# Weight splits for attention during the projections, and context attention's first products ahead of x's Fourier input

## The chip, the cores and the metric

The kernel runs on one core of one Trainium2 chip. The metric is the device time of one execution in microseconds (us), the median of several. The engines are TensorE (PE, matmuls), VectorE (DVE), ScalarE (ACT), GpSimd (POOL) and SyncE (SP), which in this kernel issues all transfers through one queue, in order.

## The reference

Two layers of a hybrid block work on 512 tokens x and 256 context tokens ctx, model width 1024. In each layer a modulated input goes through one projection of 1440 columns, and the columns go to four groups: latent attention (MLA), spatial gating, multi-scale pooling and Fourier mixing. The results are joined and go through an output projection, a residual layer norm and a SwiGLU network. Context tokens use the same weights but see only themselves; in the second layer they supply only keys and values. Cut to what matters here:

```python
cq = rms_norm(proj[..., OFF_Q:OFF_KV], q_norm)
ckv = rms_norm(proj[..., OFF_KV:OFF_KR], kv_norm)
q = (cq @ w_uq).reshape(B, L, N_HEADS, QK_NOPE + QK_ROPE)      # 8 heads, 64 + 32
k_nope = (ckv @ w_uk).reshape(B, L, N_HEADS, QK_NOPE)
v = (ckv @ w_uv).reshape(B, L, N_HEADS, V_DIM)
...
attn = blocked_attend(q, concat([k_c, k]), concat([v_c, v]))
mix = concat([attn, spatial_gating(...), multiscale_pool(...), fourier_mix(...)])
if not last:
    attn_c = attend(q_c, k_c, v_c)
    mix_c = concat([attn_c, ...])
```

Everything is float32 and the order of the groups within a layer is free, as long as what they read is there.

## The kernel before

A product in float32 accuracy is made of three matmuls in a rounded format (`mm3`, L172 to L174). For that every operand is split into a high and a low part: ACT casts the value (L168), and DVE, for some tiles POOL, subtracts that from the value (L169). A weight tile comes into a staging tile `s` (pool `sp`, four buffers), usually 512 KB, and is split into a tile `w` (pool `wp`, five buffers). A staging buffer is free when the subtraction has read it; a `w` buffer when the last matmul has read it.

The program is written as a sequence of stages, and a planner orders the instructions of each engine; every engine then works strictly in that order. In the first layer `inproj` makes the first products (its last columns are the queries' and keys' latents, `at`). `chunk_b` projects the two halves of spatial gating: accumulators `pd` and `ps`, then a layer norm on DVE of the second half (L374 and L376 statistics, L530 and L533 scaling, L169 the split of the result) with small steps on POOL between. `chunk_d` projects the pooling group with the weight halves D0 and D4 (named by the first k tile of each), `chunk_c` the Fourier group with C0 and C4, context tokens first, then x. Then come `pool_sums` on DVE and POOL, `spatial` (transposes L819, products, and L814, which multiplies the gate), `pool_proj`, and attention.

Beside this runs the computation of the next modulation (`mods`): 512 KB tiles of `w_mod` are loaded into the same four staging buffers (L260) and multiplied, unsplit, with the condition vectors (L274, four matmuls of each 128 rows of `w_mod`), then follow a sum with the bias (L280), transposes (L293) and copies into `modT` (L298, L300). Its instructions are put among the other matmuls by `fill`. A tile of `w_mod` keeps its staging buffer until its L274 matmuls are done.

`qkv_weights` (L605 to L624) loads `w_uk` and `w_uv` into one staging tile and the two halves of `w_uq` into two more, scales them by the norm's gains (L607, L617), splits them and copies parts of the query weights on POOL (L624). The three `w` tiles stay in use until attention ends. `make_ckv` and `make_cq` transpose and split the latents, `make_k` and `make_q` make keys of a head pair and the query of a head, `values` the values. `attention` is a generator that yields after each step of one head: `scores`, the keys of the next pair, the query of the next head, the transposes of an earlier step (`turn`) and the weighted sum of one still earlier (`weigh`). In layer 0 attention of the context runs interleaved with the generator `fourier`. `chunk_c` was called as a function, and `fill(99)` runs out what is left of `mods`.

## Time and profile before

| | us |
|---|---|
| median of three runs | 1672.93 (1671.89 to 1675.65) |
| the profiled execution | 1668.66 |
| its span | 1666.9 |
| PE busy | 1572.3 (94%) |
| DVE busy | 1045.8 (63%) |
| ACT busy | 769.3 (46%) |
| POOL busy | 260.6 (16%) |
| mean granted clock | 0.984 |

PE is busy in nearly all of the span, but busy time of pipelined matmuls overlaps, so what counts in a stretch is where PE stands and what it then waits for. The timeline shows it: an instruction's row ends with the idle time ahead of it and its releaser. The stretch of layer 0 that matters here lies from 100 to 245 us, that of layer 1 from 1056 to 1110 us. Times of starts are counted from the span's start.

### The profile page before, as it was taken

What the parts mean: (1) busy time and instruction counts of PE and PEld (TensorE: products, weight loads), DVE (VectorE), ACT (ScalarE), POOL (GpSimd) and SP (SyncE); (2) the same over time, 40 slices, a digit from 0 to 9 for tenths busy, and PEclk for the clock granted to TensorE, in tenths of its full rate; (3) what the DMA queues carried; (4) which work ended last, traced back from release to release, by engine and by line L of the source; (5) the groups of instructions that cost most, each with busy time, mean ns of one, the idle gap of its engine ahead of it and who ended that gap; (6) DMA issues with size and microseconds to landing.
All of it is one profiled execution on the core that took longest, in us unless ns stands there. A gap on an engine that the chain in (4) does not pass through costs nothing.

```text
span 1666.9 us, 23834 instructions
## 1 busy us (share of the span) xinstructions
PE 1572.3 (94%) x9129; PEld 1358.9 (82%) x9129; DVE 1045.8 (63%) x1591; ACT 769.3 (46%) x1371; POOL 260.6 (16%) x322
## 2 busy tenths in 40 slices
PE   6999889999999999999999798989999899998997
PEld 3856778888899999997766487879988899997786
DVE  1443676876766666664544437677857778886835
ACT  2521675884633434344232516368845445554220
POOL 0213011330000000000305005433311000001402
PEclk9999999999999999999999799999999999999999
DMA  9566114128322333449876726411156244457321
GB/s 327 178 218 202 39 39 140 46 81 279 110 82 93 94 95 101 130 133 338 315 257 226 222 67 200 145 33 39 39 176 197 76 127 127 127 177 266 119 82 58
DMA packets 180502, 241.80 MB, mean 145 GB/s; under 512 B 10874, under 2 KB 127468, under 8 KB 180388
## 3 DMA queue, kind: packets, MB, share of 16 engines
q1 hardware_dynamic: 180388, 240.28, 44.8%
q8 instruction: 72, 1.18, 0.3%
q14 instruction: 42, 0.34, 0.1%
HBM read 215.30 MB, written 24.94 MB: 144 GB/s over the span
## 4 chain that ended last, share of the span: by engine, by line
PE 81%; DVE 8%; DMA 4%; ACT 4%; issue 2%; SPq 0%; POOL 0%; POOLq 0%; DVEq 0%; ACTq 0%
PE pd L1187 21%; PE pd L172 10%; PE pd L173 10%; PE pd L174 10%; PE ps L172 5%; PE ps L173 5%; PE ps L174 5%; PE ps L1187 4%; PE ps L274 3%; PE ps L731 3%; PE ps L715 2%; DVE w L169 2%; DVE u L169 2%; DMA u<-in_w_mod_dram 1%; DMA s<-in_w_ffn_dram 1%
## 5 line engine op out<-in xcount | busy, mean ns | idle before, releaser
L168 ACT CAST w<-s 128x1024 fp32r<-128x1024 f32 (+3 forms) x285 | 292.7, 1031 | 473.0 <-PE pd L1187 141.2
L169 DVE TENSOR_TENSOR w<-s,w 128x1024 fp32r<-128x1024 f32 (+3 forms) x285 | 352.5, 1244 | 195.8 <-ACT w L168 195.7
L1187 PE MATMUL pd<-u,w 128*128 128x256 f32 (+1 forms) x1938 | 295.4, 308 | 19.0 <-DVE w L169 14.3
L1187 PEld LDWEIGHTS pd<-u,w 128*128 128x128 f32 x1938 | 282.7, 191 | 25.2 <-DVE w L169 15.8
L172 PE MATMUL pd<-w,u 128*128 128x512 f32 (+5 forms) x728 | 277.9, 383 | 8.3 <-DVE u L169 3.6
L173 PE MATMUL pd<-w,u 128*128 128x512 f32 (+5 forms) x728 | 274.3, 377 | 1.7 <-DVE w L169 1.7
L174 PE MATMUL pd<-w,u 128*128 128x512 f32 (+5 forms) x728 | 272.9, 376 | 0.0
L172 PEld LDWEIGHTS pd<-w,u 128*128 128x128 f32 x728 | 140.3, 193 | 54.6 <-issue 16.3
L173 PEld LDWEIGHTS pd<-w,u 128*128 128x128 f32 x728 | 140.3, 193 | 29.3 <-issue 5.9
L174 PEld LDWEIGHTS pd<-w,u 128*128 128x128 f32 x728 | 140.2, 193 | 27.2 <-issue 4.2
L168 ACT CAST u<-y 128x512 fp32r<-128x512 f32 (+2 forms) x178 | 94.2, 546 | 61.5 <-DMA y<-yd 28.4
L169 DVE TENSOR_TENSOR u<-y,u 128x512 fp32r<-128x512 f32 (+2 forms) x118 | 77.7, 679 | 63.0 <-ACT u L168 61.8
L169 POOL TENSOR_TENSOR u<-y,u 128x512 fp32r<-128x512 f32 (+1 forms) x60 | 78.9, 1323 | 225.5 <-ACT u L168 203.2
L172 PE MATMUL ps<-u,w 128*128 128x256 f32 (+2 forms) x288 | 92.1, 328 | 1.8 <-DVE modT L300 1.1
L174 PE MATMUL ps<-u,w 128*128 128x256 f32 (+2 forms) x288 | 93.5, 327 | 0.0
L173 PE MATMUL ps<-u,w 128*128 128x256 f32 (+2 forms) x288 | 93.3, 326 | 0.1
L172 PE MATMUL ps<-w,u 128*128 128x512 f32 (+1 forms) x208 | 81.2, 398 | 5.6 <-DVE u L169 4.7
L169 DVE TENSOR_TENSOR u<-ps,u 128x512 fp32r<-128x512 f32 (+2 forms) x106 | 66.7, 654 | 28.8 <-ACT u L168 27.8
L173 PE MATMUL ps<-w,u 128*128 128x512 f32 (+1 forms) x208 | 82.0, 395 | 1.4 <-DVE w L169 1.4
L174 PE MATMUL ps<-w,u 128*128 128x512 f32 (+1 forms) x208 | 81.4, 393 | 0.0
L1304 POOL TENSOR_TENSOR f<-f,f 128x1024 f32<-128x1024 f32 x10 | 25.8, 2598 | 333.5 <-DMA f<-rd 254.4
L1187 PE MATMUL ps<-u,w 128*128 128x384 f32 (+1 forms) x456 | 75.3, 313 | 0.0
(250 smaller groups left out, 2579.5 us busy)
## 6 DMA issues: line engine op xcount, KB each, us to landing
s<-in_w_ffn_dram SPq DMA_DIRECT2D x154, 512.0 KB
s<-in_w_out_dram SPq DMA_DIRECT2D x50, 512.0 KB
u<-in_w_mod_dram SPq DMA_DIRECT2D x48, 512.0 KB
s<-in_w_mod_dram SPq DMA_DIRECT2D x48, 512.0 KB
s<-in_w_in_dram SPq DMA_DIRECT2D x16, 512.0 KB
yd<-f SPq DMA_DIRECT2D x19, 384.0 KB
y<-yd SPq DMA_DIRECT2D x88, 64.0 KB
y<-yd SPq DMA_DIRECT2D x22, 256.0 KB
```

Source lines behind the costliest of these rows:

```text
L168: A_.copy(out=hi, in_=src)
L169: (eng or V_).tensor_tensor(out=lo, in0=src, in1=f(hi), op=ALU.subtract)
L172: T_.matmul(ps, lhsT=ll, rhs=rh, start=start, stop=False)
L173: T_.matmul(ps, lhsT=lh, rhs=rl, start=False, stop=False)
L174: T_.matmul(ps, lhsT=lh, rhs=rh, start=False, stop=stop)
L274: T_.matmul(ps[32 * j:32 * j + 32, :n], lhsT=sst[:, k, :], rhs=ws[j // 2][:, (j % 2) * n:(j % 2 + 1) * n], start=(k == 0), stop=(k == KD - ...
L715: T_.transpose(pt[:, o:o + P], es[t2][:, k * P:(k + 1) * P], ident)
L731: T_.matmul(av[:, 0:256], lhsT=vt[k][:, h, :], rhs=pts[k // 2][:, a, (k % 2) * 256:(k % 2 + 1) * 256], start=(k == 0 and a == 1), stop=(k ...
L1187: T_.matmul(ps, lhsT=A[u][:, k], rhs=B[k][:, v], start=first and k == 0 and i == 0, stop=last and k == 3 and i == 2, skip_group_check=True)
L1304: G_.tensor_tensor(out=y, in0=y, in1=bc[0], op=ALU.mult)
```

## The change

Three edits. First, `wkv, wq = qkv_weights(l)` is called straight behind `chunk_b`, ahead of `chunk_d`, in both layers; before, it came behind `make_ckv`. Second, `chunk_c` becomes a generator that yields after each stream. In layer 0, when the context's part is done, `make_cq(C)` is called, context attention is created and its first part runs: the keys of the first pair and the first two queries. Only then follows x's part of `chunk_c`, and then `fill(99)`. Third, the generator of context attention makes its queries two heads ahead, and yields once more, behind these first products. Lines behind the edits have moved down (L607 is L608, L617 is L618, L814 is L820, L866 is L872).

```diff
@@ chunk_c
             v = lambda ap: ap.rearrange("p n c -> p (n c)")
             split(v(st.f[0]), v(st.f[1]), pd[:, :n])
+            yield
@@ attention
         make_k(0, wkv, st)
         q[0] = make_q(st, 0, wq)
+        qa = 1
+        if st.s:
+            q[1] = make_q(st, 1, wq)
+            qa = 2
+            yield
         for i, (h, qp) in enumerate(steps):
...
-            if qp == 0 and h < NH - 1:
-                q[h + 1] = make_q(st, h + 1, wq)
+            if qp == 0 and h < NH - qa:
+                q[h + qa] = make_q(st, h + qa, wq)
@@ hybrid_kernel, the loop over layers
         chunk_b(l, act)
+        wkv, wq = qkv_weights(l)
         pts = chunk_d(l, act)
...
         make_ckv(C, at)
         if l == 1:
             make_ckv(X, at)
-        wkv, wq = qkv_weights(l)
+        vt = []
         if l == 1:
             make_cq(X, at)
-        chunk_c(l, act)
+        cc = chunk_c(l, act)
+        if l == 0:
+            next(cc)
+            make_cq(C, at)
+            ac = attention(C, vt, wkv, wq)
+            next(ac)
+        run(cc)
         fill(99)
-        if l == 0:
-            make_cq(C, at)
-        vt = []
         fo = fourier(l, act)
         if l == 0:
             values(wkv, vt, range(NTC))
-            ac = attention(C, vt, wkv, wq)
```

Where the instructions went, by the order that the planner gives each engine. SP in layer 0, the transfers at the end of `chunk_b`, before (`s` is a staging buffer with its tile's number, `in_w_in` the input projection's weights: D4, C0 and C4):

```order
L260 DMA s_138_940<-in_w_mod_dram 128x1024
L186 DMA s_159_1040<-in_w_in_dram 128x4x256
L186 DMA s_161_1045<-in_w_in_dram 128x4x256
L186 DMA s_163_1050<-in_w_in_dram 128x4x256
L260 DMA s_169_1074<-in_w_mod_dram 128x1024
L286 DMA gd<-y_1057 2x512 x2
```

and now:

```order
L606 DMA s_159_1040<-in_w_uk_dram 128x512
L607 DMA s_159_1040<-in_w_uv_dram 128x512
L615 DMA s_161_1047<-in_w_uq_dram 128x768
L615 DMA s_164_1063<-in_w_uq_dram 128x768
L186 DMA s_167_1079<-in_w_in_dram 128x4x256
L186 DMA s_169_1084<-in_w_in_dram 128x4x256
L243 DMA y_1107<-in_b_mod_dram 2x512
L286 DMA gd<-y_1096 2x512 x2
L243 DMA y_1107<-in_b_mod_dram 2x512 x3
L872 DMA y_1406<-in_w_pool_dram 64x64 x4
L186 DMA s_171_1089<-in_w_in_dram 128x4x256
L260 DMA s_177_1113<-in_w_mod_dram 128x1024
```

Three transfers of attention weights stand ahead of D4, and the next `w_mod` tile stands behind C4 instead of behind three transfers. DVE at the same place, from the last statistics of `chunk_b` on (`i` and `pd`, `ps` are its tiles and accumulators), before:

```order
L376 BN_AGGR st_1031<-bn_1029 128x2
L530 SCALAR_TENSOR_TENSOR i_968<-pd_731,st_1006,y_964 128x256
L530 SCALAR_TENSOR_TENSOR i_1016<-ps_732,st_1020,y_964 128x256
L530 SCALAR_TENSOR_TENSOR i_1016<-ps_733,st_1031,y_964 128x256
L533 SCALAR_TENSOR_TENSOR i_968<-i_968,st_1006,y_964 128x256
L533 SCALAR_TENSOR_TENSOR i_1016<-i_1016,st_1020,y_964 128x256
L533 SCALAR_TENSOR_TENSOR i_1016<-i_1016,st_1031,y_964 128x256
```

and now, with the scalings (L618) and subtractions (L169 from `s_161` and `s_164`) of the query weights, and D4's from `s_167`:

```order
L618 TENSOR_SCALAR s_161_1047<-s_161_1047,st_1049 128x768
L530 SCALAR_TENSOR_TENSOR i_968<-pd_731,st_1006,y_964 128x256
L618 TENSOR_SCALAR s_164_1063<-s_164_1063,st_1065 128x768
L530 SCALAR_TENSOR_TENSOR i_1016<-ps_732,st_1020,y_964 128x256
L530 SCALAR_TENSOR_TENSOR i_1016<-ps_733,st_1031,y_964 128x256
L169 TENSOR_TENSOR y_1412<-y_1406,y_1412 128x256
L533 SCALAR_TENSOR_TENSOR i_968<-i_968,st_1006,y_964 128x256
L169 TENSOR_TENSOR w_163_1052<-s_161_1047,w_163_1052 128x8x96
L533 SCALAR_TENSOR_TENSOR i_1016<-i_1016,st_1020,y_964 128x256
L533 SCALAR_TENSOR_TENSOR i_1016<-i_1016,st_1031,y_964 128x256
L169 TENSOR_TENSOR w_166_1068<-s_164_1063,w_166_1068 128x8x96
L169 TENSOR_TENSOR w_168_1080<-s_167_1079,w_168_1080 128x1024
```

The query weights' scalings and subtractions stand among and behind the norm's last steps, and D4's subtraction, which stood ahead of the norm, behind them. PE at the same place is the same in both but for tile numbers; now:

```order
L174 MATMUL ps_733<-w_128_851,u_589 128x512
L293 MATMUL ps_1100<-ident,y_1096 128x128 x4
L274 MATMUL ps_1117<-s_177_1113,sst 32x512 x2
L172 MATMUL ps_1130<-u_287,w_134_908 128x512
L173 MATMUL ps_1130<-u_287,w_134_908 128x512
L174 MATMUL ps_1130<-u_287,w_134_908 128x512
```

The last matmul of `chunk_b`, four transposes, the L274 on the `w_mod` tile `s_177`, and the first of `chunk_d` kept their places. DVE in `spatial` of layer 0, before, with the splits of x's and the context's results behind it:

```order
L814 SCALAR_TENSOR_TENSOR i_967<-ps_1300,PV,i_967 128x4x64
L846 SCALAR_TENSOR_TENSOR i_1265<-i_1266,ic,i_1159 128x784
L814 SCALAR_TENSOR_TENSOR i_967<-ps_1305,PV,i_967 128x4x64
L814 SCALAR_TENSOR_TENSOR i_967<-ps_1310,PV,i_967 128x4x64
L814 SCALAR_TENSOR_TENSOR i_967<-ps_1315,PV,i_967 128x4x64
L169 TENSOR_TENSOR u_1287<-ps_1320,u_1287 128x512
```

and now:

```order
L820 SCALAR_TENSOR_TENSOR i_967<-ps_1339,PV,i_967 128x4x64
L820 SCALAR_TENSOR_TENSOR i_967<-ps_1344,PV,i_967 128x4x64
L169 TENSOR_TENSOR w_271_1709<-s_270_1708,w_271_1709 128x1032
L820 SCALAR_TENSOR_TENSOR i_967<-ps_1349,PV,i_967 128x4x64
L820 SCALAR_TENSOR_TENSOR i_967<-ps_1354,PV,i_967 128x4x64
L169 TENSOR_TENSOR w_273_1714<-s_272_1713,w_273_1714 128x1032
L169 TENSOR_TENSOR u_1326<-ps_1359,u_1326 128x512
```

The two subtractions of the Fourier table (128x1032) moved among the four multiplications of x.

## Rows read from the trace of the kernel before

**Rows 1.** The page, chain that ended last, share of the span by engine:

```profile
PE 81%; DVE 8%; DMA 4%; ACT 4%; issue 2%; SPq 0%; POOL 0%; POOLq 0%; DVEq 0%; ACTq 0%
```

**Rows 2.** Timeline of PE, 104 to 116: start, us, operation, count, idle before.

```profile
111.87 0.60 PE L293 MATMUL ps<-ident,y 128*128 128x128 f32 x4
112.66 1.05 PE L274 MATMUL ps<-s,sst 128*32 128x512 f32 x4 [0.19 <-DMA s<-in_w_mod_dram]
114.82 0.47 PE L172 MATMUL ps<-u,w 128*128 128x512 f32 x1 [1.10 <-DVE modT L300]
```

**Rows 3.** Timeline of PE, 170 to 245: instructions with idle time ahead.

```profile
179.33 0.39 PE L172 MATMUL pd<-w,u 128*128 128x258 f32 x1 [1.77 <-DVE u L169]
191.04 0.36 PE L172 MATMUL ps<-kT,u 96*128 96x256 f32 x1 [1.00 <-DVE u L169]
195.96 0.35 PE L172 MATMUL ps<-kT,u 96*128 96x256 f32 x1 [1.62 <-DVE u L169]
```

**Rows 4.** Busy by stretch: length, PE, PEld, DVE, ACT, POOL, granted clock, DMA, GB/s.

```profile
170.00:180.00 10.00, 6.73 (x42) 4.98 (x41) 8.81 (x23) 8.79 (x18) 0.00 (x0) 1.00 0.31 106
180.00:182.50 2.50, 2.50 (x14) 2.50 (x13) 1.42 (x4) 0.00 (x0) 1.17 (x2) 0.50 0.00 0
182.50:185.00 2.50, 2.50 (x16) 2.37 (x16) 0.00 (x0) 0.28 (x1) 0.00 (x0) 0.82 0.00 0
197.50:200.00 2.50, 2.50 (x15) 2.50 (x13) 1.27 (x4) 2.02 (x7) 0.00 (x0) 0.50 0.00 0
```

**Rows 5.** Timeline of SP, 100 to 125: transfers as issued.

```profile
101.13 6.47 SPq L186 DMA_DIRECT2D s<-in_w_in_dram  x3
107.69 0.46 SPq L260 DMA_DIRECT2D s<-in_w_mod_dram  x1
```

**Rows 6.** Timeline of ACT, 104 to 130: the cast of D4.

```profile
104.90 1.05 ACT L168 CAST w<-s 128x1024 fp32r<-128x1024 f32 x1 [10.87 <-DMA s<-in_w_in_dram]
```

**Rows 7.** Timeline of DVE, 156 to 162: query weights scaled and subtracted.

```profile
157.16 0.70 DVE L617 TENSOR_SCALAR s<-s,st 128x768 f32<-128x768 f32 x1
157.78 2.62 DVE L169 TENSOR_TENSOR w<-s,w 128x768 fp32r<-128x768 f32 x1
...
160.81 0.94 DVE L169 TENSOR_TENSOR w<-s,w 128x768 fp32r<-128x768 f32 x1
```

**Rows 8.** Timeline of DVE, 104 to 126: norm of `chunk_b` and what stands among it.

```profile
107.72 0.69 DVE L280 TENSOR_TENSOR y<-ps,y 128x512 f32<-128x512 f32 x1 [0.51 <-PE ps L274]
...
110.64 0.43 DVE L374 BATCH_NORM_STATS2 bn<-pd 128x6 f32<-128x256 f32 x1
...
112.64 1.22 DVE L169 TENSOR_TENSOR w<-s,w 128x1024 fp32r<-128x1024 f32 x1
...
118.95 0.24 DVE L376 BATCH_NORM_AGGREGATE st<-bn 128x2 f32<-128x6 f32 x2
...
119.48 0.86 DVE L530 SCALAR_TENSOR_TENSOR i<-ps,st,y 128x256 f32<-128x256 f32 x2
...
121.18 0.99 DVE L533 SCALAR_TENSOR_TENSOR i<-i,st,y 128x256 f32<-128x256 f32 x2 [0.44 <-POOL st L368]
```

**Rows 9.** Timeline of POOL, 150 to 175: what ran beside the longer subtraction.

```profile
157.53 2.06 POOL L833 TENSOR_TENSOR i<-i 64x784 f32<-64x784 f32 x1
```

**Rows 10.** Timeline of DVE, 169 to 172: the Fourier table's first subtraction.

```profile
169.34 1.23 DVE L169 TENSOR_TENSOR w<-s,w 128x1032 fp32r<-128x1032 f32 x1 [0.21 <-ACT w L168]
```

**Rows 11.** Timeline of PE, 155 to 172: two matmuls that follow each other.

```profile
155.10 0.28 PE L172 MATMUL pd<-w,u 128*128 128x256 f32 x1
155.22 0.29 PE L173 MATMUL pd<-w,u 128*128 128x256 f32 x1
```

**Rows 12.** Timeline of PE, 1059 to 1069: the start of `chunk_d` in layer 1.

```profile
1067.57 0.39 PE L172 MATMUL ps<-u,w 128*128 128x512 f32 x1
1067.80 0.39 PE L173 MATMUL ps<-u,w 128*128 128x512 f32 x1
```

**Rows 13.** Timeline of DVE, 1056 to 1083: query weights in layer 1.

```profile
1074.67 0.61 DVE L617 TENSOR_SCALAR s<-s,st 128x768 f32<-128x768 f32 x1
...
1078.05 0.94 DVE L169 TENSOR_TENSOR w<-s,w 128x768 fp32r<-128x768 f32 x1
```

## The prediction

> **What bounds the kernel now.** I read the chain that ended last first: PE holds 81% of the span, DVE 8%, DMA 4% [rows 1]. So TensorE's stream of matmuls sets the end nearly everywhere, and a change counts by the idle time that it puts into that stream or takes out of it. Then the timelines of the stretch that the change touches. In layer 0 PE works without a hole from the weight projection of `chunk_b` into that of `chunk_d` except for two short waits: 0.19 us before an L274 matmul, for the transfer of a `w_mod` tile, and 1.10 us before the first matmul of `chunk_d` [rows 2]. From then on it has no idle time until 171 us. The holes come at the hand-over to attention: 1.77 us before the first matmul of x's Fourier input, at 179.33, then 1.00 and 1.62 us among the first heads of context attention [rows 3]. After these idle stretches the granted clock is at 0.50, its lower level of 1.2 GHz, from 180 to 182.5 and from 197.5 to 200 [rows 4]. That is the loss that the second and third edit can get back; the first edit works where there is almost nothing to get back.
>
> **Split of key, value and query weights, layer 0.** No arithmetic is added: the same three loads, scalings, casts and subtractions come earlier. Before, they stood at 153 to 161 us beside other work of PE. Now they take three of four staging buffers just as the last weights of `chunk_b` leave them, so everything that SP issues behind them is late. The order shows this: D4, C0, C4 and the next `w_mod` tile were issued from 101.13 to 107.69 [rows 5]; now uk+uv and the two halves of uq stand there, C4 waits for the staging buffer of the first half of uq and that `w_mod` tile for the second, and a staging buffer is free only when DVE has done the subtraction that ends its split. PE's order is not changed at this place: its first instruction after `chunk_b` and four transposes is the L274 matmul on exactly this tile, and all matmuls of `chunk_d` are queued behind it.
>
> When is the second subtraction done? DVE works in order, and it now stands behind nearly all of `chunk_b`'s layer norm. I walk along DVE with the durations of before. uk+uv land about when the first w_in tile did, its cast started at 104.90 and took 1.05 [rows 6]; with scaling 0.75, estimated from the 0.70 of the smaller one [rows 7], and subtraction 1.23 DVE is at 107.9, then L280, 0.69 [rows 8]: 108.6. The first of the four accumulators is complete at about 109.1, so the norm starts there, not at 110.64 as now. From its first BATCH_NORM_STATS2 to the end of the last BATCH_NORM_AGGREGATE it takes 110.64 to 119.19 now, with a weight subtraction of 1.22 among it that is gone from there: 7.3 [rows 8], so 116.4. Then two scalings of 0.70 [rows 7], three L530 of about 0.44, the pool weights' subtraction, which I put at 0.44 like the L530 beside it, and one L533 of about 0.48 [rows 8]: 3.6, so 120.0. First query subtraction 0.94, two L533 0.99, second subtraction 0.94 [rows 7, 8]: 122.9, about 122.6 since instructions of one engine overlap by some hundredths each. Issue to use of a 512 KB tile is 104.90 - 101.13 = 3.8 [rows 5, 6]. The L274 matmul can start at 126.4. PE is ready at 112.66 - 0.19 = 112.5 [rows 2]. Stall 13.9, of which the 0.19 and 1.10 of before go off: **+12.6**. The nearest cover would be other matmuls ahead of this L274 in PE's order, and there are none. Bounds: the tile may land in 3.0, nearer to an idle queue, and the norm be shorter by 1: +10.6; and both query subtractions may be stretched as one of two was, 2.62 in place of 0.94 [rows 7]: +16.
>
> That 2.62 stands beside a POOL subtraction of 2.06 that began 0.25 before it [rows 7, 9]. By the Trainium skill, SBUF — State Buffer, section "SBUF: two separate sides", VectorE with two SBUF inputs and GpSimd reading SBUF hold one port pair by an exclusive lock, for a whole instruction. The row agrees: from the end of the POOL instruction, 159.59, another 0.9 leads to the end of the DVE one. By this rule the new place has only short POOL instructions beside the subtractions, a stretch of tenths and a sum near mine; by the row alone it would be 3.4 more. I take the undisturbed 0.94, from the row to which the undisturbed case is nearest, and keep 3.4 in the range.
>
> After such a stand the clock will be low for a stretch. Nearest rows: after idle time at the hand-over, 2.5 us at 0.50 and 2.5 at 0.82 [rows 4], that is 1.25 + 0.45 = **+1.7**; bounds 0 (were the clock to stay up) and 4 (as long again at 0.50).
>
> The rest of `chunk_d` and `chunk_c` follows behind: 15 `w_mod` tiles come one for one as L274 matmuls free buffers, as now; I see waits of some tenths. The three split weights also stay in three of five `wp` buffers, so D0, D4, C0 and C4 share two; C0's cast waits for D0's last matmul. Some 0.4 us, within the bounds above.
>
> **Spatial, layer 0.** Of the 96 x matmuls of `chunk_c` 65 stood behind the first matmul of `spatial` and filled PE while DVE and ScalarE went round; now 9 do. Nothing is saved by that: the 56 others, of 0.12 us each [rows 11], are done earlier, in a row, and 6.6 us of cover are gone. Also, the two subtractions of the Fourier table, 1.23 each [rows 10], come among the first L820 (L814 before), behind casts of 1.05 that themselves wait for the last use of C0 and C4. I take one cast and two subtractions, 1.05 + 2.46 = **+3.5**; bounds 0 (the transfer and the cast come early enough) and 6.6.
>
> **Context attention ahead, layer 0.** `make_k(0)` and two `make_q` now stand before x's Fourier input and give PE 2 to 3 us of matmuls there, and each later head finds its query two steps old. The three waits named sum to 1.77 + 1.00 + 1.62 = 4.4 [rows 3], the two dips of the clock cost 1.7 and 1.25 [rows 4]: 7.4 in all is the ceiling. But the waits are for splits that pass through ScalarE and DVE, which are busy for 8.8 of the 10 us from 170 to 180 [rows 4], and no work is taken off either; after the first few heads the order of PE is as before. Nothing tells how much of it comes back, so I take the half: **-3.7**, bounds -1 and -7.4.
>
> **Layer 1.** Same move. PE enters `chunk_d` at 1067.57 and has 24 matmuls, one each 0.23 [rows 12], 5.6 us, that need only the first half of its weights. Then it needs D4, whose subtraction stands behind the second half of the norm, from the last accumulator on about 3.3, the last steps of [rows 8] at the same durations, two scalings of 0.61, an L533 of 0.5, two subtractions of 0.94 [rows 13] and its own 1.22: 8.1. So **+2.5**; bounds 0 and 5. Here no L274 stands at the front.
>
> **Sum** against the profiled execution, 1668.66: 12.6 + 1.7 + 3.5 - 3.7 + 2.5 = +16.6, 1685.3. That execution lies 4.3 below the median of the runs, 1672.93; on the median the same difference gives 1689.5.
>
> **Rivals.** (a) The stall is smaller. If the planner's order is met by a tile that lands early, or by a norm that runs much ahead of my walk, the stall at `chunk_d` is 6 to 8, the clock and layer 1 cost 1 together, spatial stays covered, the gain stays: 7 + 1 - 3.7 = +4.3, 1677. For: `w_mod` tiles otherwise land ahead of use. Against: two engines' orders tie the tile to the second subtraction. (b) Faster, the other side: uk, uv and uq land while `chunk_b` still runs on PE, and the splits end before the norm. The deciding point is whether the second query subtraction ends before about 109, which leaves 3.8 for the transfer by 112.8; then no stall and no dip, and the hand-over gives up to 7.4 less 2.5 of layer 1: -4.9, 1668. Against: the norm stands ahead of both in DVE's order, and its last accumulator is complete only at 112. (c) Deeper: both query subtractions stretched by 1.7, a clock that stays low for longer, spatial's 6.6: +16 + 4 + 6.6 - 2 + 4 = +29 at most, likely +24, 1697. (d) The edit does nothing: the build moves these instructions on four engines, so only a cancelling of terms gives no change, 1673.
>
> **How the numbers follow.** Forecast 0.66, (a) 0.13, (b) 0.07, (c) 0.10, (d) 0.04. What a measurement can tell from no change is 0.2%, 3.3 us: below 1669.6 is faster, above 1676.3 slower. (b) is faster; (a) is slower but for a little; so faster 0.08, same 0.06, slower 0.86. The range leaves out (b), (d) and the low half of (a), and the top of (c): 1679 to 1698.
>
> **What would show it.** In the profile of the changed kernel: one wait of PE at L274 for DMA `w_mod` of about 14 us, begun at 112 to 113; SP issuing that tile at about 122.5, just behind the second query subtraction; a granted clock of 0.5 for a slice behind 126; waits of 1 to 2 us at the spatial transposes; the first heads' waits smaller than in [rows 3]; about 2.5 us at a DVE subtraction in layer 1 behind 1073. I am wrong if that L274 waits under 6 us, if attention's waits shrink by over 8, or if PE's waits elsewhere grow by more than they do here.

## The result, and the profile of the changed kernel

The changed kernel takes **1692.28 us** (median of 4 runs, 1688.51 to 1694.91) against 1672.41 (1671.48 to 1675.65) for the kernel before, measured beside it: a ratio of 1.0117, interval 1.0100 to 1.0135. It is slower, by 19.9 us where +16.6 was forecast. The profiled execution took 1694.77, near the top of its four runs, with a span of 1693.0 (1666.9 before) and a mean granted clock of 0.978 (0.984 before).

The chain that ended last, by engine, answers to [rows 1]: PE has lost three points of its share, DVE and DMA have gained one each.

```profile
PE 78%; DVE 9%; DMA 5%; ACT 4%; issue 2%; SPq 0%; POOL 0%; POOLq 0%; DVEq 0%; ACTq 0%
```

PE's timeline at the end of `chunk_b` in layer 0 answers to [rows 2] (start, us, operation, count, idle before and its releaser):

```profile
112.61 0.60 PE L293 MATMUL ps<-ident,y 128*128 128x128 f32 x4
127.24 1.92 PE L274 MATMUL ps<-s,sst 128*32 128x512 f32 x4 [14.03 <-DMA s<-in_w_mod_dram]
129.09 0.79 PE L172 MATMUL ps<-u,w 128*128 128x512 f32 x1
```

The 0.19 before the L274 has become 14.03; the 1.10 before the first matmul of `chunk_d` is gone, since `modT` has long been ready. Why the transfer is late is read from SP and DVE together. SP at the same place, against [rows 5]:

```profile
105.37 3.35 SPq L615 DMA_DIRECT2D s<-in_w_uq_dram  x2
108.81 0.94 SPq L186 DMA_DIRECT2D s<-in_w_in_dram  x2
...
121.19 0.37 SPq L186 DMA_DIRECT2D s<-in_w_in_dram  x1
122.89 1.51 SPq L260 DMA_DIRECT2D s<-in_w_mod_dram  x2
```

DVE, against [rows 7, 8]:

```profile
107.25 1.23 DVE L169 TENSOR_TENSOR w<-s,w 128x1024 fp32r<-128x1024 f32 x1 [1.11 <-ACT w L168]
...
110.00 0.43 DVE L374 BATCH_NORM_STATS2 bn<-pd 128x6 f32<-128x256 f32 x1 [0.85 <-PE pd L174]
...
117.11 0.24 DVE L376 BATCH_NORM_AGGREGATE st<-bn 128x2 f32<-128x6 f32 x2
...
120.21 0.96 DVE L169 TENSOR_TENSOR w<-s,w 128x768 fp32r<-128x768 f32 x1
121.08 0.88 DVE L533 SCALAR_TENSOR_TENSOR i<-i,st,y 128x256 f32<-128x256 f32 x2
121.87 2.17 DVE L169 TENSOR_TENSOR w<-s,w 128x768 fp32r<-128x768 f32 x2
```

The first query subtraction ends at 121.17, and C4 (L186) is issued at 121.19. The second begins at 121.87 and shares its row with D4's, which is a group of two; the `w_mod` tile is issued at 122.89, about 1.0 after it began. From there to the L274 are 4.35 us. PE, SP and DVE stand in one ring, and the norm of `chunk_b` is in it.

The windows (length; busy PE, PEld, DVE, ACT, POOL; granted clock; DMA share; GB/s), against [rows 4]:

```profile
120.00:130.00 10.00, 2.76 (x6) 1.04 (x7) 5.16 (x9) 2.48 (x7) 8.09 (x19) 0.50 0.50 157
...
130.00:132.50 2.50, 2.50 (x11) 1.95 (x11) 0.00 (x0) 0.00 (x0) 0.00 (x0) 0.87 0.67 206
132.50:135.00 2.50, 2.50 (x12) 1.12 (x10) 0.00 (x0) 0.00 (x0) 0.00 (x0) 1.00 0.01 3
...
180.00:182.50 2.50, 2.50 (x24) 2.50 (x23) 1.15 (x3) 1.06 (x1) 0.00 (x0) 1.00 0.02 7
...
187.50:190.00 2.50, 2.30 (x12) 1.81 (x11) 1.20 (x3) 1.28 (x3) 0.00 (x0) 0.73 0.43 148
190.00:192.50 2.50, 2.50 (x11) 1.93 (x9) 1.38 (x3) 2.50 (x7) 0.00 (x0) 0.59 0.00 0
...
197.50:200.00 2.50, 2.50 (x16) 1.96 (x15) 1.67 (x5) 2.30 (x6) 0.00 (x0) 1.00 0.00 0
```

The clock is at 0.50 (1.2 GHz) in the stall and for 2.76 us of work behind it, then 0.87 and 1.00. The two stretches that stood at 0.50 before, at 180 and 197.5, are now at 1.00; the work that stood in them comes some 10 to 17 us later, and its waits have shrunk. But a new dip stands at spatial's end, 0.73 and 0.59 from 187.5 to 192.5; the repeat of this kernel has 1.00 there. PE's waits at spatial's end and the hand-over to attention, against [rows 3]:

```profile
184.21 0.66 PE L825 MATMUL ps<-ident,i 128*128 128x128 f32 x4 [0.35 <-DVE i L820]
186.08 0.33 PE L172 MATMUL ps<-i,u 128*128 128x128 f32 x1 [0.93 <-DVE u L169]
...
196.06 0.36 PE L172 MATMUL ps<-u,w 128*128 128x256 f32 x1 [0.57 <-DVE kT L169]
217.25 0.39 PE L172 MATMUL ps<-kT,u 96*128 96x256 f32 x1 [0.53 <-DVE u L169]
220.31 0.74 PE L732 MATMUL ps<-u,u 128*128 128x256 f32 x4 [0.74 <-DVE kT L169]
```

No wait is over 1 us any more where there were 1.77, 1.00 and 1.62.

**Where the 26 us between the two profiled executions lie.** Four matmuls that stand in all traces cut the span: the wait for the exponentials in x's attention of layer 0, the first 128x416 matmul of layer 1, the same exponentials there, and the end. In the changed kernel:

```profile
254.28 0.45 PE L172 MATMUL pd<-kT,u 128*128 128x384 f32 x1 [1.04 <-ACT e L686]
...
1048.32 0.71 PE L172 MATMUL pd<-w,u 128*128 128x416 f32 x1 [0.95 <-DVE u L169]
...
1134.03 0.44 PE L172 MATMUL pd<-kT,u 128*128 128x384 f32 x1 [1.03 <-ACT e L686]
```

In the kernel before the same three start at 243.53, 1031.51 and 1113.20. The stretches (us) for all profiled executions, one trace each, and the granted clock of the first 36 us of layer 1:

| kernel | to the first | to layer 1 | layer 1 (clock at its start) | rest | weights moved in layer |
|---|---|---|---|---|---|
| before | 243.5 | 788.0 | 81.7 (1.00) | 553.7 | none |
| changed | 254.3 | 794.0 | 85.7 (0.95) | 559.0 | 0 and 1 |
| changed, again | 254.2 | 789.6 | 87.0 (0.95) | 556.6 | 0 and 1 |
| ahead only | 238.6 | 789.1 | 81.3 (1.00) | 556.0 | none |
| move only | 258.8 | 788.6 | 87.6 (0.94) | 556.2 | 0 and 1 |
| move in layer 0 | 261.2 | 791.8 | 83.1 (0.95) | 557.4 | 0 |
| move in layer 1 | 244.0 | 787.5 | 86.4 (0.94) | 555.1 | 1 |
| one query ahead | 239.3 | 785.7 | 83.2 (0.94) | 557.7 | none |
| fill first | 260.1 | 788.7 | 84.0 (1.00) | 555.4 | 0 and 1 |
| queries behind `chunk_d` | 240.8 | 791.1 | 82.8 (0.95) | 554.2 | keys and values alone |
| all behind `chunk_d` | 238.4 | 785.7 | 83.7 (0.93) | 558.5 | less far, both |
| query halves in other buffers | 246.2 | 789.9 | 86.7 (0.93) | 553.1 | 0 and 1 |
| all weights in other buffers | 248.5 | 787.7 | 86.2 (0.95) | 558.7 | 0 and 1 |
| behind `chunk_d` in layer 0 | 238.5 | 785.6 | 83.7 (0.93) | 556.4 | less far, 0 |

The first column follows the edits, and so does the third within one clock. The second and fourth, where nothing was edited, spread over 8.5 and 5.9 us whatever the kernel. Of the 26.1 us, 10.8 are in the first column (0.7 of them already there when `chunk_b` ends, ahead of the first wait that the change makes), 4.0 in the third, and 6.1 and 5.3 in stretches for which the repeat gives 1.6 and 2.9. One trace against another says less than the medians do: before's profiled execution lies 4.3 under its median, the changed kernel's 2.5 above.

### The profile page after: what moved, and what is told of

Its sections match the earlier page's. It is cut to its first block, busy times and chain, and to the rows that moved or that the text cites. A ratio compares the mean times of both kernels' runs of the same rounds, so it can differ in the third digit from the quotient of the medians.

```text
span 1693.0 us, 23834 instructions
## 1 busy us (share of the span) xinstructions
PE 1575.4 (93%) x9129; PEld 1358.6 (80%) x9129; DVE 1045.0 (62%) x1591; ACT 770.2 (45%) x1371; POOL 264.8 (16%) x322
## 4 chain that ended last, share of the span: by engine, by line
PE 78%; DVE 9%; DMA 5%; ACT 4%; issue 2%; SPq 0%; POOL 0%; POOLq 0%; DVEq 0%; ACTq 0%
PE pd L1193 20%; PE pd L172 10%; PE pd L173 9%; PE pd L174 9%; PE ps L172 6%; PE ps L173 5%; PE ps L174 5%; PE ps L274 3%; PE ps L1193 3%; DVE w L169 3%; PE ps L732 3%; PE ps L716 2%; DVE u L169 2%; ACT w L168 2%; DMA s<-in_w_ffn_dram 2%
## 5 line engine op out<-in xcount | busy, mean ns | idle before, releaser
L169 DVE TENSOR_TENSOR w<-s,w 128x1024 fp32r<-128x1024 f32 (+4 forms) x285 | 351.8, 1242 | 244.4 <-ACT w L168 243.9
L168 ACT CAST w<-s 128x1024 fp32r<-128x1024 f32 (+4 forms) x285 | 292.3, 1030 | 447.7 <-PE pd L1193 121.7
L1193 PE MATMUL pd<-u,w 128*128 128x256 f32 (+1 forms) x1938 | 300.9, 308 | 20.7 <-DVE f L1235 10.1
L172 PEld LDWEIGHTS pd<-w,u 128*128 128x128 f32 x728 | 138.4, 190 | 58.3 <-issue 18.9
L173 PEld LDWEIGHTS pd<-w,u 128*128 128x128 f32 x728 | 138.4, 190 | 31.9 <-issue 6.7
L174 PEld LDWEIGHTS pd<-w,u 128*128 128x128 f32 x728 | 138.2, 190 | 25.4 <-issue 2.5
L169 DVE TENSOR_TENSOR u<-y,u 128x512 fp32r<-128x512 f32 (+2 forms) x118 | 79.1, 692 | 65.8 <-ACT u L168 64.2
L169 POOL TENSOR_TENSOR u<-y,u 128x512 fp32r<-128x512 f32 (+1 forms) x60 | 80.2, 1343 | 226.0 <-ACT u L168 207.6
L169 DVE TENSOR_TENSOR u<-ps,u 128x512 fp32r<-128x512 f32 (+2 forms) x106 | 66.7, 655 | 33.4 <-ACT u L168 32.4
L1193 PE MATMUL pd<-u,f 128*128 128x384 f32 (+1 forms) x456 | 74.0, 312 | 0.0
```

The costliest lines, as they stand in the source:

```text
L168: A_.copy(out=hi, in_=src)
L169: (eng or V_).tensor_tensor(out=lo, in0=src, in1=f(hi), op=ALU.subtract)
L172: T_.matmul(ps, lhsT=ll, rhs=rh, start=start, stop=False)
L173: T_.matmul(ps, lhsT=lh, rhs=rl, start=False, stop=False)
L174: T_.matmul(ps, lhsT=lh, rhs=rh, start=False, stop=stop)
L1193: T_.matmul(ps, lhsT=A[u][:, k], rhs=B[k][:, v], start=first and k == 0 and i == 0, stop=last and k == 3 and i == 2, skip_group_check=True)
```

## The experiments

Each ran beside the kernel before, on the same chip; ratios are against it, with 95% intervals.

**Ahead only**: the second and third edit, the weights at their old place.

```diff
         chunk_b(l, act)
-        wkv, wq = qkv_weights(l)
         pts = chunk_d(l, act)
...
             make_ckv(X, at)
+        wkv, wq = qkv_weights(l)
         vt = []
```

> Edits two and three without the first: the weights are split where they were before, behind make_ckv. Theory: the loss sits in the early split alone, so the wait of the L274 matmul at 112 us is back under 1 us, the short waits at the start of context attention shrink, and the time is 1667 to 1672 (1 to 5 under before). Rival (the products ahead of x's Fourier input cost something of their own, by later weights for them or lost cover): 1675 or more, with new waits of PE between 150 and 200 us.

Measured 1667.95, ratio 0.999 (0.998 to 1.000). PE lists no L274 wait in `chunk_b`'s last part, and `chunk_d` starts as before:

```profile
114.46 0.47 PE L172 MATMUL ps<-u,w 128*128 128x512 f32 x1 [1.36 <-DVE modT L300]
```

The first column falls by 4.9, to 238.6: the second and third edit do what they are for, and only 2.6 of that reaches the medians (1670.56 before), so little that the interval of the ratio ends at 1.000.

**Move only**: the first edit alone, in both layers.

```diff
         chunk_b(l, act)
+        wkv, wq = qkv_weights(l)
         pts = chunk_d(l, act)
...
             make_ckv(X, at)
-        wkv, wq = qkv_weights(l)
```

> The first edit alone, in both layers; chunk_c and attention as before. Theory: wait of about 14 us at L274, about 3 us in layer 1, no gain at attention: 1690 to 1697. Rival (the loss needs the attention edits too): under 1685.

Measured 1694.87, ratio 1.0165 (1.0146 to 1.0184). PE's waits in layer 0:

```profile
126.87 1.92 PE L274 MATMUL ps<-s,sst 128*32 128x512 f32 x4 [14.28 <-DMA s<-in_w_mod_dram]
...
195.61 0.58 PE L172 MATMUL pd<-w,u 128*128 128x258 f32 x1 [1.53 <-DVE u L169]
207.86 0.35 PE L172 MATMUL ps<-kT,u 96*128 96x256 f32 x1 [1.00 <-DVE u L169]
212.77 0.36 PE L172 MATMUL ps<-kT,u 96*128 96x256 f32 x1 [1.61 <-DVE u L169]
```

The stall and the three waits of [rows 3] stand side by side. So the stall belongs to the first edit, and the smaller waits in the changed kernel to the others.

**Move in layer 0 only, and in layer 1 only**: the same diff under `if l == 0` or `if l == 1`, the old call for the other layer.

> The first edit alone and in layer 0 only. Theory: the wait of 14 us at L274 stays, layer 1 is as before: 1685 to 1691, and 3 to 5 less than the first edit in both layers. Rival (what the trace shows beyond the stall, +5 in the first layer's feed-forward network and +5 at the end, belongs to the change): 1692 or more.

> The first edit alone, in layer 1 only. Theory: one wait of PE of 2 to 3 us at the start of chunk_c or chunk_d there, nothing else: 2 to 4 over before. Rival (it is hidden, and what layer 1 lost in the changed kernel came from a low clock carried in from before): within 1 of before.

Layer 0 alone: 1692.72, ratio 1.0139 (1.0124 to 1.0154), with the L274 wait at 14.08. That is not the 1685 to 1691 of the theory but the time of its rival: more is lost than the stall and its clock account for. Layer 1 alone: 1672.95, ratio 1.0020 (1.0006 to 1.0034), as the theory had it. Together they make 1.6%, as the move in both does (1.65%). PE's waits in layer 1 of the second:

```profile
1077.59 0.38 PE L172 MATMUL pd<-w,u 128*128 128x256 f32 x1 [2.22 <-ACT w L168]
1085.99 0.38 PE L173 MATMUL pd<-w,u 128*128 128x256 f32 x1 [0.55 <-DVE w L169]
```

In that trace ACT and DVE show what came late (same columns), first ACT:

```profile
1073.77 2.52 ACT L168 CAST w<-s 128x768 fp32r<-128x768 f32 x3 [0.15 <-DVE s L617]
...
1076.50 1.04 ACT L168 CAST w<-s 128x1024 fp32r<-128x1024 f32 x1
```

then DVE:

```profile
1074.64 3.04 DVE L169 TENSOR_TENSOR w<-s,w 128x768 fp32r<-128x768 f32 x3
```

The matmul that waits in name is the first of `chunk_c`, which stands among those of `chunk_d` and needs C0's cast, the last row of ACT. But D4's subtraction, the third of DVE's group, ends at 1077.68, 0.14 later than that cast, and the next matmul, on D4, starts at 1077.82. Both chains lead through the query halves behind the norm and end together; either alone would have cost the 2.2. The 24 matmuls of `chunk_d` before the wait begin at 1069.63, 38.1 after the first 128x416 matmul where it was 36.1 before: that is the lower clock at the start of layer 1.

**One query ahead**: the weights at the old place, and context attention makes only its first keys and first query ahead.

```diff
@@ attention (weights at the old place)
         qa = 1
         if st.s:
-            q[1] = make_q(st, 1, wq)
-            qa = 2
             yield
```

> The second edit alone: weights where they were before, one query ahead as before, only the first keys and the first query stand ahead of x's Fourier input. Theory (the start of attention, not the two heads of lead, is what gains): PE's first scores of head 1 come 3 to 5 us earlier than before and the time is within 1 us of that with both edits. Rival (the second query ahead carries it): the waits of 1.0 and 1.6 us at the first scores stay, and PE is at most 2 us ahead of before at 243.5.

Measured 1667.72, ratio 0.9987 (0.9974 to 1.0000); the first column is 239.3, 0.7 above that of both edits. The rival is out: with one query ahead, too, the waits of 1.00 and 1.62 at the first scores have gone down to 0.24 and 0.53. Nearly all that is gained comes from the first products standing ahead of x's Fourier input; the second query ahead is worth less than a measurement can tell.

**Fill first**: all edits, and `fill(1)` ahead of the weights, so that the `w_mod` tile doesn't stand behind them.

```diff
         chunk_b(l, act)
+        fill(1)
         wkv, wq = qkv_weights(l)
```

> All three edits, but one step of the modulation is issued ahead of the weights, so two w_mod tiles have staging buffers before uk and uq take theirs; the splits stand where the change puts them. Theory (the staging buffer that the w_mod tile waits for is the cause): the L274 matmul waits under 1 us, PE goes on with 24 matmuls that need only the first half of chunk_d's weights, and then waits 0 to 3 us for D4's subtraction: 1674 to 1680, the rest being layer 1. Rival (DVE's queue is the cause whatever is loaded first, since D4's subtraction stands behind the norm): a wait of 6 to 12 us, now at DVE, and 1684 or more.

Measured 1697.76, ratio 1.0159 (1.0136 to 1.0182); the profiled execution, 1690.0, is the fastest of four, so its trace shows less than the loss of the median. The time is that of the rival, not the 1674 to 1680 of the theory. The L274 wait at the front is gone and the loss is not:

```profile
114.51 0.47 PE L172 MATMUL ps<-u,w 128*128 128x512 f32 x1 [0.35 <-DVE modT L300]
122.67 0.58 PE L172 MATMUL ps<-u,w 128*128 128x256 f32 x1 [5.13 <-ACT i L532]
142.78 2.28 PE L274 MATMUL ps<-s,sst 128*32 128x512 f32 x5 [3.69 <-DMA s<-in_w_mod_dram]
```

PE now runs into `chunk_d` and waits 5.13 for an accumulator of `chunk_b`. The norm has yet to read it, and ACT's copy that does (L532) stands behind the casts of the query halves. The other `w_mod` tiles, issued only from 124.35 on, come one at a time: a wait of 2.62 and seven more of 0.47 to 1.21 follow. They have two of the four staging buffers, since C0 and C4 hold the others until their casts, and these wait for PE to be done with another split weight (pool `wp`):

```profile
173.71 1.05 ACT L168 CAST w<-s 128x1024 fp32r<-128x1024 f32 x1 [32.46 <-PE ps L174]
```

The windows of that stretch show the price of such single waits in the clock:

```profile
140.00:150.00 10.00, 4.20 (x12) 0.52 (x12) 1.03 (x2) 0.92 (x2) 0.85 (x5) 0.80 0.63 207
150.00:160.00 10.00, 6.55 (x14) 0.75 (x16) 0.00 (x0) 0.00 (x0) 0.00 (x0) 0.50 0.60 179
160.00:170.00 10.00, 6.90 (x16) 0.56 (x12) 0.68 (x1) 0.00 (x0) 0.00 (x0) 0.50 0.49 161
```

The order of one transfer is thus not the whole cause: the staging buffers as a whole are held, and with them the norm's own steps on ScalarE.

**Query halves behind `chunk_d`**: key and value weights stay behind `chunk_b`, the query halves are loaded and split behind `chunk_d`.

```diff
         chunk_b(l, act)
-        wkv, wq = qkv_weights(l)
+        wkv = kv_weights(l)
         pts = chunk_d(l, act)
+        wq = q_weights(l)
```

> As the changed kernel, but only the key and value weights are split behind chunk_b; the two halves of the query weights follow behind chunk_d, in both layers. Theory (the w_mod tile waits for the staging buffer of a query half, whose subtraction stands behind the norm): that buffer is now the one of the key and value weights, free at about 108, so the L274 matmul waits under 1 us and the time is 1666 to 1671, near that of edits two and three alone. Rival (three loads and splits in one stretch are too much for SP and DVE wherever they stand, or the key and value tile alone does it): L274 still waits 4 us or more, 1675 to 1690.

Measured 1669.0, ratio 0.9994 (0.9984 to 1.0005).

```profile
115.24 1.05 PE L274 MATMUL ps<-s,sst 128*32 128x512 f32 x4 [3.42 <-DMA s<-in_w_mod_dram]
```

The time is that of the theory; the wait is not. It is 3.42, between what theory (under 1) and rival (4 or more) gave, and the clock does not fall behind it (1.05, not 1.92, for the L274). DVE's subtraction for uk and uv ended at 107.14, as the theory had it, so the staging buffer was free then. SP shows what the tile waited for instead:

```profile
109.57 1.55 SPq L243 DMA_DIRECT2D y<-in_b_mod_dram  x3
111.22 2.33 SPq L260 DMA_DIRECT2D s<-in_w_mod_dram  x3
```

In SP's order the six small transfers from 107.98 to 111.12 (the last three are shown) now stand ahead of it, where it was issued at 107.69 before, ahead of them [rows 5]. So the 3.42 is SP's order, and the 10.6 by which the wait falls from 14.03 is the part of the query halves.

**All behind `chunk_d`**: all three edits, but the call of `qkv_weights` behind `chunk_d`, in both layers.

```diff
         chunk_b(l, act)
-        wkv, wq = qkv_weights(l)
         pts = chunk_d(l, act)
+        wkv, wq = qkv_weights(l)
```

> As the changed kernel, with all three attention weights split behind chunk_d instead of behind chunk_b, in both layers. Theory: no L274 wait, layer 1 without the 2.2 us wait for a cast, the gain at attention stays: 1665 to 1669. Rival (early weights hold three of five split buffers and starve chunk_c and the Fourier table, wherever in the projections they are split): new waits of PE for ACT or DVE at w between 130 and 200 us, 1672 or more.

Measured 1668.05, ratio 0.9977 (0.9964 to 0.9990), though the medians themselves differ by 1.3 alone (1669.35 before); the L274 waits 0.28, and the gain of the other edits is whole (238.4).

**Other buffers for the query halves, and for all three weights**: after this, the weights stay where the change put them, but are loaded into another pool, so that they hold no staging buffer. The first kernel has the second hunk alone, the second both.

```diff
@@ qkv_weights
-        st4 = S4(D)
+        st4 = U(n=D)
...
-            st4 = S4(768)
+            st4 = U(n=768)
```

> The changed kernel with one word different: the two halves of the query weights are loaded into tiles of another pool, not into staging buffers. Their scalings and subtractions stay where the change puts them on DVE, and D4's subtraction stays behind them. Theory (two things lie behind the 14 us, the buffer and DVE's queue): the w_mod tile now waits for the key and value weights' buffer only, the L274 wait falls to 2 to 4, as with the query weights behind chunk_d; a second wait of 3 to 6 comes a few matmuls later, for an accumulator or for D4: 1676 to 1684. Rival (the buffer alone): no second wait, 1667 to 1673. Rival (DVE's queue alone): 1686 or more.

> The same with the key and value weights too in the other pool, so D4, C0, C4 and w_mod have the staging buffers to themselves, as before. Theory: the L274 wait is under 1 us, and what is left is DVE's queue: one wait of 4 to 8 at the second accumulator of chunk_d or at D4: 1674 to 1682. Rival (the queue costs nothing once the buffers are free): 1665 to 1670.

Query halves: 1678.93, ratio 1.0062 (1.0046 to 1.0078). All three: 1680.81, ratio 1.0072 (1.0057 to 1.0088). Against the changed kernel's 1690.26 beside them some 10 us come back, and 8 to 10 don't. PE's waits of the first and of the second kernel:

```profile
116.55 1.92 PE L274 MATMUL ps<-s,sst 128*32 128x512 f32 x4 [3.35 <-DMA s<-in_w_mod_dram]
122.37 1.05 PE L274 MATMUL ps<-s,sst 128*32 128x512 f32 x4 [0.34 <-DMA s<-in_w_mod_dram]
```

```profile
114.22 1.05 PE L274 MATMUL ps<-s,sst 128*32 128x512 f32 x4 [0.50 <-DMA s<-in_w_mod_dram]
119.21 1.05 PE L274 MATMUL ps<-s,sst 128*32 128x512 f32 x4 [0.96 <-DMA s<-in_w_mod_dram]
124.16 1.92 PE L274 MATMUL ps<-s,sst 128*32 128x512 f32 x4 [3.89 <-DMA s<-in_w_mod_dram]
```

The times are those of the theories, the waits only in part. In the first kernel the second wait of 3 to 6 did not come (0.34), and the 3.35 is SP's order again: the tile is issued at 112.60, 0.10 behind the same small transfers. In the second, with no attention weight in a staging buffer, the third L274 still waits 3.89, and PE is busy for 1.11 of the 5 us from 120 to 125. Its tile is issued at 120.31, just when the second L274 has ended, so one staging buffer goes round for all `w_mod` tiles. The others are held: D4's until its subtraction, which begins only at 123.69, behind the norm and both query subtractions, and those of C0 and C4 until 146 to 149, because their casts wait for a split buffer:

```profile
143.81 1.04 ACT L168 CAST w<-s 128x1024 fp32r<-128x1024 f32 x1 [0.83 <-PE ps L174]
```

Three of the five split buffers are with the attention weights by then. For D4 itself PE doesn't wait: its subtraction has ended at 124.94, and PE gets to it at 128.74. So the staging buffers of the attention weights are some 10 us of the loss. Of the 8 to 10 that are left, the first column has 2.7 and 4.9, layer 1 the 4.5 to 5.0 that the move costs there too; in the first column SP's order, DVE's order and the split buffers are what the traces name. A kernel with more split buffers, which would tell their share, was not run. In layer 1 a wait of 1.76 and 1.81 remains at C0's cast, as it must if ScalarE's and VectorE's orders make it and not a staging buffer.

**Layer 0 behind `chunk_d`, layer 1 at the old place**: the cheapest place of each.

```diff
         chunk_b(l, act)
-        wkv, wq = qkv_weights(l)
         pts = chunk_d(l, act)
+        if l == 0:
+            wkv, wq = qkv_weights(l)
...
             make_ckv(X, at)
+        if l == 1:
+            wkv, wq = qkv_weights(l)
```

> All three edits, with the weights split behind chunk_d in layer 0 and at their old place in layer 1. Theory: as with chunk_d in both layers, since layer 1 showed the same waits with either: 1664 to 1669. Rival (the earlier place in layer 1 was worth something): 1669 or more.

Measured **1666.07** against 1670.58, ratio 0.9978 (0.9962 to 0.9993): with all weights behind `chunk_d` in both layers (1668.05, 0.9977) it is one of two versions whose interval lies below 1, by 0.2%. Their intervals overlap with that of ahead only, so whether the moved weights add anything to its gain can't be told.

**The changed kernel again**, beside the last three.

> The changed kernel once more, for its spread and a second trace. Theory: the 5 to 6 us that its first trace lost between 254 and 1031 us, at one wait of 3.7 for a cast, do not belong to the change, since its instructions there stand in the same order: the second trace has 14 at L274 and 2.8 in layer 1 again, but under 2 there, and the median is 1688 to 1692. Rival (they belong to it, by the shifted start of the feed-forward weights' transfers): the wait is there again, over 3 us.

Measured 1690.26 (1688.4 to 1694.35), ratio 1.0132 (1.0111 to 1.0153), as the theory had it; the L274 waits 14.12, layer 1 shows 2.23 and 0.54, and the wait for a cast between 254 and 1031 us that was 3.7 is 1.2 here. So 2.5 of the 6.1 by which the first trace's second column grew are that one wait, and not the change.

## Why the prediction was right

**The ring around the L274: right, and to 0.1 us.** Predicted 13.9, measured 14.03; less the 1.10 and the 0.19 that go, +12.7 against +12.6. The steps of the walk: the uk+uv subtraction ended at 108.48 (107.9 in the walk), the norm ran from 110.00 to 117.35 (109.1 to 116.4: its start waited 0.85 for an accumulator, since all of this trace is 0.7 later at this place), the second query subtraction ended at about 122.8 (122.6). The transfer took 4.35 to its use, not 3.8, and PE was ready 0.7 later than in the walk, which cancel: the 0.1 is in part luck. The choice of the undisturbed 0.94 for the query subtractions held: 0.96 for the first, and 2.17 for the second with D4's, 0.94 + 1.22 at the durations of before. POOL was busy beside them, for 8.09 of the 10 us from 120, with short instructions, the first of a row of twelve and a later group of four:

```profile
120.26 1.00 POOL L625 CAST w<-w 128x64 fp32r<-128x64 f32 x1
...
127.32 0.76 POOL L625 CAST w<-w 128x64 fp32r<-128x64 f32 x4
```

The four at 127.32 stand alone and take 0.76 in all, the first of them 0.23. The cast at 120.26 begins 0.05 behind the first query subtraction and takes 1.00; one behind the second subtraction takes 0.96, one behind D4's 1.23, and each ends within 0.1 of the end of that subtraction. The subtractions (0.96, 1.00 and 1.25) grew by hundredths. [rows 7, 9] show the other order: a POOL instruction of 2.06 began first, and the subtraction took 1.7 longer, near the 1.8 that the POOL instruction had left to run. By the Trainium skill, SBUF — State Buffer, section "SBUF: two separate sides", whichever of the two engines starts first keeps the shared ports for its whole instruction. The traces agree in both directions. So the choice of 0.94 was right, and what made it so is that POOL came second, and that its instructions are short besides.

**The clock: right.** Predicted +1.7; by the windows 2.76 us of work at 0.50 and 2.5 at 0.87 give 1.38 + 0.33 = 1.7. Between that L274 and spatial the profile lists no other wait of PE, and the stretch is longer by 1.6 once the work that moved into it and the 1.10 of before are taken off: the clock is what it lost. In the repeat 4.20 us of work stand at 0.50 and 2.5 at 0.90, which makes 2.4.

**Spatial: mis-sized, and for another reason: +3.5 against +1.8.** From spatial's first transposes to the first query transposes (L599) the change took 192.22 - 176.44 = 15.78, before 175.35 - 153.60 = 21.75. What moved out of this stretch is counted by `chunk_c`'s matmuls in it, in the first row before, in the second now (one of three such groups each):

```profile
L174 PE MATMUL pd<-w,u 128*128 128x256 f32 x37 | 10.5, 284 | 0.0
L174 PE MATMUL pd<-w,u 128*128 128x256 f32 x15 | 4.2, 280 | 0.0
```

In all 110 have become 44 (the 65 and 9 of the prediction are counted from spatial's first product, which comes later). The 66 others, at 0.118 each, are 7.8 us, and 15.78 against 21.75 - 7.8 is +1.8; the repeat gives 15.34, +1.4. The subtractions of the Fourier table do stand among the L820s, but PE's waits there, 0.35, 0.93 and 0.20, sum to what they were before (0.3, 0.8 and 0.4), and the 1 to 2 us forecast at the transposes did not come. The step that failed is the one that put a cast and two subtractions on the path: DVE had 2.96 us of idle time ahead of the first L820. What grew in this trace is the clock's part: behind those waits it fell to 0.73 and 0.59 where it stood at 1.00 before, some 1.6 us on the 4.80 of work in these two windows. In the repeat the clock stayed up, and PE waited 0.89 for a cast at L599 instead. That the lost cover is behind either is likely, but no run shows it.

**Attention: right in its sign, mis-sized, -3.7 against -6.1.** From L599 to the first matmul of x's keys the change took 52.82, before 58.93. The half that was taken for want of a better number was too little: the waits for splits that pass through ScalarE and DVE did shrink, and both clock dips of before went. The repeat gives 54.02, -4.9, and ahead only 53.97, -5.0, so the true size is nearer to 5 than to the 7.4 of the ceiling. The wait of 1.77 that the prediction put at x's Fourier input is at the first product of `fourier`, a stage later (its 258 columns are those of the Fourier table, where the projection has 256).

**Layer 1: right.** Predicted +2.5 at D4's subtraction. The two waits sum to 2.8 (2.22 and 0.54 to 0.55), less some 0.2 of waits further on: +2.6. D4's subtraction and C0's cast, which the walk left out, end within 0.14 of each other. The other 1.4 of the changed kernel's 4.0 lie ahead of `chunk_d`, where the clock is 0.95. That isn't the move's doing as far as the traces go: the kernels without it show it too (one query ahead 0.94, behind `chunk_d` in layer 0 0.93). At a clock of 1.00 the third column is 81.3 and 81.7 without the move and 84.0 with it; at 0.93 to 0.95 it is 83.1 to 83.7 and 85.7 to 87.6.

**The sum: right in total, in part by luck.** 12.7 + 1.7 + 1.8 - 6.1 + 2.6 is +12.7, under the +16.6. The medians differ by 19.7 to 19.9, so some 7 us have no place in these terms, and it is the +3.5 at spatial and the -3.7 at attention, too high by 1.7 and 2.4, that brought the forecast nearer to the time. (The lower bound of the first term, too, was added up wrongly, +10.6 for +10.8.) The 7 us lie in stretches that the change doesn't edit: 0.7 ahead of the stall, the start of layer 1, and the second and fourth column. Taking the first and third column's growth off the growth of the median leaves 3.1 to 8.4 us for the five kernels with a stall at their front (changed, its repeat, move only, move in layer 0, fill first) and -1.5 to 2.7 for the eight others. That speaks for the rival of move in layer 0: some 3 us more are lost behind a layer 0 that comes late. The size is an estimate, with one trace each, and by which mechanism no trace shows: this stays open. Rival (b), that the splits end before the norm, failed at its deciding point: the second query subtraction began at 121.87, where it had to end before 109.

**The gain that doesn't arrive.** The ahead edits take 4.9 us from layer 0 and leave 2.6 in the median. In the trace of the ahead-only kernel PE waits 7.11 in the last feed-forward stretch for a weight subtraction, where before's trace has 1.43 there and 5.92 some 50 us earlier. One could take it that PE, being early, outruns its weights. But the same wait stands at 6.4 to 7.3 in twelve of the fourteen traces, also in those that come there some 20 us late (6.39 in the changed kernel), so being early is not its reason. Before and query halves in other buffers, the two without it, have the shortest last columns, 553.7 and 553.1. Where the rest of the gain goes stays open; part of it is that before's trace is a fast one.

## What to carry to other kernels

Before loads are moved earlier, walk the whole ring: buffer held until which engine's instruction, which stands behind what in that engine's order (a cast that must first get a split buffer included), and what is queued ahead of and behind the load in the issuing queue; here a step of 0.94 us on an engine with idle time cost 14 us on the one that sets the end, because it stood behind a norm that waits for that same engine's matmuls. Every engine that the moved work passes through has its own order to be walked. The same loads one stage later, behind the matmuls that need the buffers, cost nothing that these runs can tell and kept the gain.

## What the runs showed of the hardware

A stand of 14 us costs more than itself: the granted clock was 0.50 for 2.76 us of work behind it (4.20 in the repeat), and L274's group of four took 1.92 where it takes 1.05 at full clock. A wait of 3.42 (queries behind `chunk_d`) left the clock up, with an L274 of 1.05; one of 3.35 in the kernel with other buffers did not, 1.92. A row of waits of about 1 us each between short groups of matmuls kept the clock at 0.50 for 20 us (fill first, 150 to 170). A POOL cast of 0.23 us took 0.96 to 1.23 when it began just behind a VectorE subtraction, which itself lost hundredths; a subtraction that began 0.25 behind a POOL instruction of 2.06 took 2.62 for 0.94. And stretches fed by weight transfers, which no edit touched, varied between 785.6 and 794.0 us from trace to trace across these kernels, more than the 4.9 that the edits to attention gain.
